# The 1/rms of two stages, taken from the input rows and applied to the projections' products; the rope tables loaded ahead of the gated stage

## The chip, the cores and the metric

The kernel runs on one core of a Trainium2 chip. The metric is device time in microseconds (us), as the median of several executions. The engines of a core work side by side, each through its own instruction queue: PE (TensorE, matrix products and transposes), DVE (VectorE), ACT (ScalarE), POOL (GpSimd) and SP, which here only issues DMA transfers. PEld is PE's loading of weights, which overlaps its products.

## The reference, cut to what matters

A sequence of 256 rows with 1024 features passes a first block (two layers of mixed attention) and a second block (a gated stage, then a dilated attention). Only the second block is touched. In float32:

```
x = first_block(...)
for i in (0, 1):                                  # gated, dilated
    h = x * rsqrt(mean(x*x, axis=-1) + 1e-6) * norm_pre[i]
    y = gated(h) if i == 0 else dilated(h)
    x = x + rms_norm(y) * norm_post[i]

gated(h):    p = h @ w_in                         # 1024 -> 6144
             u, v = split(gelu(p[:, :4096])); z = p[:, 4096:]
             v = layer_norm(v)                    # over 2048
             sv = tril(w_s[g]) @ v + b_s[g]       # per 128 rows, group g of 8
             return (u * sv * silu(z)) @ w_out
dilated(h):  p = h @ w_in                         # 3 groups of q, k, v and one z
             q, k = rope(q, cos, sin), rope(k, cos, sin)
             o_g = softmax(mask(q k / 8)) v; o = sum_g alpha_g o_g
             return (o * silu(z)) @ w_out
```

The factor 1/rms is one number per row of x. A product h @ w has it as a factor per row too.

## The kernel before

**Tiling.** The 256 rows are two row blocks (`tb` 0 and 1) of 128 partitions. A float32 product is made as three matrix products of split numbers: `mm3` (L184) multiplies hi by hi (L193), lo by hi (L194) and hi by lo (L195) for each of 8 pieces of 128 features. Weights arrive by DMA (`raw`, issued by SP at L158), are rounded by ACT (`whi`, L172) and the remainder is taken by POOL (`wlo`, L175) or DVE (`wlo`, L177). SP sends its transfers in the order written.

**From rows to the products' left side.** `make_h_gain` (L257) runs once per row block at each of two boundaries: at the end of the first block (L783) for the gated stage, and at the end of the gated stage (L884) for the dilated one. It takes 1/rms by `row_rstd` (ACT squares and sums the two halves at L232, DVE adds the two sums into `hst` at L234, POOL computes mean plus epsilon at L202 and the power -0.5 at L204). DVE then forms `xh`, the row times 1/rms times the gain, in two halves of 512 (L264). PE transposes each half (`hps`, L269), ACT rounds it to the hi part (`hxh`, L271) and DVE takes the lo part (`hxl`, L272).

**Gated stage** (`gmlp`, L810). Four slabs of v for each block (Gelu at L838, statistics at L839), the layer norm on DVE (L846 to L848), then 8 groups with u (Gelu, L860), z (Tanh of half of it, L862), DVE products at L863 to L866, and the output product.

**Dilated stage** (`dilated`, L888). It loads mask and rope tables at its start. 8 passes (`pair`, L1033) with two heads each: q and k are projected, rotated with the tables (L915 to L917), transposed and split (L924 to L928); v is split in three bf16 parts (`split_v`, L293); z goes through Tanh (L1050) and `gate` (L1052). `attend` (L931) makes scores (L331), masks them with a running maximum (DVE's own instruction at L965), exponentials (L313, with the sum `z`, completed by POOL at L316), transposes them by DMA, multiplies by v (L339 to L341) and divides by z (`rz`, L1018, applied at L1023).

**Order of the work.** In the first two stages the framework's scheduler orders every engine's instructions by its own estimates and the program's dependences; in the dilated stage PE keeps the program's order, which the small planner `Line` (L41) sets by written due times, while the other engines are still ordered by the scheduler. An engine never overtakes within its queue: what waits holds all behind it.

Of the kernel before, what the change touches and what calls it, by code (L numbers as in the profile page):

```python
# [11 lines left out]
F32 = mybir.dt.float32  # L12
# [3 lines left out]
AF = mybir.ActivationFunctionType  # L16
ALU = mybir.AluOpType
# [3 lines left out]
P = 128  # L21
# [94 lines left out]
def tile_kernel(ctx, tc, a, out):  # L116
# [139 lines left out]

    def make_h_gain(tb, act, npre):  # L257

        rs = row_rstd(xs[:, tb, :])
        hi, lo = act  # L260
        t = slice(tb * P, (tb + 1) * P)
        for hf in range(2):
            xh = s512("xh")
            nc.vector.scalar_tensor_tensor(  # L264
                xh, xs[:, tb, hf * 512 : (hf + 1) * 512], rs, npre[hf], ALU.mult, ALU.mult
            )
            ps = bank("tr", "hps", (P, 4, P))
            for j in range(4):
                nc.tensor.transpose(ps[:, j, :], xh[:, j * P : (j + 1) * P], ident)  # L269
            o = slice(4 * hf, 4 * hf + 4)  # L270
            nc.scalar.copy(hi[:, o, t], ps)  # L271
            nc.vector.tensor_tensor(lo[:, o, t], ps, hi[:, o, t].bitcast(F32), ALU.subtract)  # L272

    def row_halves(t, src):

# [14 lines left out]
            lo[:, c0 : c0 + n, t], ps[:, :n, :], scale, hi[:, c0 : c0 + n, t].bitcast(F32), ALU.mult, ALU.subtract  # L290
        )

    def split_v(dst, src, wk, eng=nc.vector):  # L293

        w = src.shape[-1]
        of = lambda t: t.rearrange("p (n m d) -> p n m d", m=dst.shape[2], d=64)
        v1, v2, v3 = (dst[:, :, :, i, :] for i in range(3))
        nc.scalar.copy(v1, of(src))
        r1 = of(wk.tile([P, 256], F32, tag="vr", bufs=1, name="vr")[:, :w])
        eng.tensor_tensor(r1, of(src), v1, ALU.subtract)  # L300
        nc.gpsimd.tensor_copy(v2, r1)
        nc.gpsimd.tensor_tensor(v3, r1, v2, ALU.subtract)

# [43 lines left out]
    def first_block():  # L347
        with ExitStack() as st:
# [327 lines left out]
            for l in range(2):  # L676
# [69 lines left out]
                if l == 0:  # L746
                    for blk in (2, 3):
                        y_out(ya, blk, (7,))
                    ya["x"] = act_tiles("x")
                    for cs_ in ((0, 1, 2, 3), (4, 5, 6)):  # L750
                        for blk in (0, 1):
                            y_out(ya, blk, cs_)
                    for blk in (0, 1):
                        attend(l, 6, "C", S, blk, lam)
                    ws = [load_w(a["w_out"][l, n]) for n in range(2)]
                    gt = gates_of(l, 1)
                    for blk in (2, 3):
                        out_proj(l, blk, ya, ws, gt, residual(l, blk))
                    gtx = gates_of(l, 0)
                    H["c"] = act_tiles("c")  # L760
                    for blk in (2, 3):
                        h_all(1, blk)
                    for blk in (0, 1):
                        y_out(ya, blk, (7,))
                    res = [residual(l, blk) for blk in (0, 1)]
                    for blk in (0, 1):
                        out_proj(l, blk, ya, ws, gtx, res[blk])
                    H["x"] = act_tiles("x")
                    for blk in (0, 1):
                        h_all(1, blk)  # L770
                else:
                    for blk in (0, 1):
                        y_out(ya, blk, (4, 5, 6))
                    gtx = gates_of(l, 0)
                    npre = row_halves(yc[0], a["npre"][0])
                    ws = [load_w(a["w_out"][l, n]) for n in range(2)]
                    hx = x_act()
                    res = [residual(l, blk) for blk in (0, 1)]
                    for blk in (0, 1):
                        attend(l, 6, "C", S, blk, lam)  # L780
                        y_out(ya, blk, (7,))
                        out_proj(l, blk, ya, ws, gtx, res[blk])
                        make_h_gain(blk, hx, npre)  # L783
                    return hx

    def post_add(tb, parts, npost, dst=None):

# [19 lines left out]
        return t  # L807


    def gmlp(hx):  # L810
        with ExitStack() as st:
            pool = lambda name, **k: st.enter_context(tc.tile_pool(name=name, **k))
            wk = pool("gwk", bufs=1)
# [17 lines left out]
            for s, tb in ((0, 0), (1, 0), (0, 1), (1, 1), (2, 0), (2, 1), (3, 0), (3, 1)):  # L831
                    if tb == 0:
                        vws[s] = load_w(a["a_w_in"][s], HALF if s < 2 else PLAIN)
                    w = vws[s]
                    pj = bank("pj", "pj")
                    mm3(pj, hx, tb, w, 0, 512)
                    c = slice(s * 512, (s + 1) * 512)
                    nc.scalar.activation(vn[tb][:, c], pj, AF.Gelu)  # L838
                    nc.vector.bn_stats(st6[tb][:, s, :], vn[tb][:, c])  # L839
            for tb in range(2):  # L840
                mv = sm.tile([P, 2], F32, tag="mv", bufs=2, name="mv")
# [8 lines left out]
            for g in range(8):  # L850
                w = load_w(a["a_w_in"][4 + g])
                for tb in range(2):
                    pj = bank("pj", "pj")
                    mm3(pj, hx, tb, w, 0, 512)
                    sv = bank("sc", "sv", (P, 256))
                    nc.tensor.matmul(
                        sv, ws[:, g, :], vn[tb][:, g * 256 : (g + 1) * 256], start=True, stop=True
                    )
                    gu = wk.tile([P, 256], F32, tag="gu", bufs=2, name="gu")
                    nc.scalar.activation(gu, pj[:, 0:256], AF.Gelu)  # L860
                    tz = wk.tile([P, 256], F32, tag="tz", bufs=2, name="tz")
                    nc.scalar.activation(tz, pj[:, 256:512], AF.Tanh, scale=0.5)  # L862
                    nc.vector.scalar_tensor_tensor(gu, sv, bs[:, g : g + 1], gu, ALU.add, ALU.mult)  # L863
                    nc.vector.scalar_tensor_tensor(tz, tz, 1.0, pj[:, 256:512], ALU.add, ALU.mult)
                    y = wk.tile([P, 256], F32, tag="gy", bufs=2, name="gy")
                    nc.vector.tensor_tensor(y, gu, tz, ALU.mult)  # L866
                    y_to_act([(y[:, i * P : (i + 1) * P], 2 * g + i) for i in range(2)], tb, ya, 0.5)
            npost = row(gp.tile([P, D], F32, name="npost"), a["npost"][0])
            pss = [[bank("sc", "ops")] for tb in range(2)]
            wo = lambda n, kh: load_w(a["a_w_out"][2 * n + kh])  # L870
            for kh in range(2):
                w = wo(0, kh)
# [3 lines left out]
            for tb in range(2):  # L876
                pss[tb].append(bank("pj", "ops"))
                for kh in range(2):
                    mm3(pss[tb][1], ya, tb, w1[kh], 0, 512, k0=8 * kh, first=(kh == 0), last=(kh == 1))
                post_add(tb, [(pss[tb][n], slice(512 * n, 512 * n + 512)) for n in range(2)], npost)  # L880
                if tb == 0:
                    h2 = x_act()
                    npre = row_halves(gp.tile([P, D], F32, name="npre"), a["npre"][1])
                make_h_gain(tb, h2, npre)  # L884
            return h2


    def dilated(hx):  # L888
        with ExitStack() as st:
            pool = lambda name, **k: st.enter_context(tc.tile_pool(name=name, **k))  # L890
            wk = pool("dwk", bufs=1)
            dp = pool("dp", bufs=1)
            mask = dp.tile([P, 1152], F32, name="mask")
            nc.sync.dma_start(mask, a["dmask"])
            rope = {}
            for nm in ("cosD", "sinD"):
                rope[nm] = dp.tile([P, 2, 64], F32, name=nm)
                nc.sync.dma_start(rope[nm], a[nm])
            ya = tuple(dp.tile([P, KC, 256], F32R, name=t) for t in ("yh", "yl"))

            def proj(w, tb, n=512):
# [29 lines left out]
            def attend(pr, tb, qk, v01, v2, gate, lead):  # L931
# [101 lines left out]
            def pair(pr, last):  # L1033
# [5 lines left out]
                def qkv(i, tb):  # L1039
                    pj = proj(ws[i], tb)  # L1040
                    fin = rotate(pj, 512 if i == 0 else 256, tb)
                    if i == 1:
                        split_v(v01[:, :, tb], pj[:, 256:512], wk)
                    turned[i, tb] = line.add(rotate_pe(fin, 4 - 2 * i, tb, qk, 2 * i), 5.0)

                def vz(tb):
                    pj = proj(ws[2], tb, 256)
                    split_v(v2[:, tb : tb + 1], pj[:, :P], wk)
                    tg = wk.tile([P, P], F32, tag="tg", bufs=1, name="tg")
                    nc.scalar.activation(tg, pj[:, P:], AF.Tanh, scale=0.5)  # L1050
# [172 lines left out]
```

## Time and profile before

| what | value |
|---|---|
| median of 3 executions | 1182.47 us (1181.87 to 1186.19) |
| profiled execution | 1193.97 us |
| its span in the trace | 1192.3 us |
| mean granted TensorE clock | 0.954 of full |
| PE busy | 1113.6 us, 93% |
| DVE busy | 837.6 us, 70% |
| ACT busy | 610.5 us, 51% |
| POOL busy | 465.8 us, 39% |
| chain of waits that ended last | PE 79%, DMA 10%, DVE 5%, ACT 2% |

The span is the time from the first to the last instruction in the trace; the profiled execution is 1.67 us longer than it. Busy time of PE is counted as busy at either clock level, so a stretch can be fully busy and still slow. In the timeline, the number in brackets is how long the engine stood idle before the instruction, and the arrow names what ended that. The second block runs from about 652 us to the end.

### The profile page before, as it was taken

The numbers are of one execution on the slowest core, as the hardware profiler recorded it, in microseconds if no ns is written. First come the engines' busy times: TensorE is split into PE (matmuls) and PEld (weight loads), VectorE is DVE, ScalarE is ACT, GpSimd is POOL, SyncE is SP. The second block draws the span as 40 slices with busy tenths as digits, with TensorE's granted clock in tenths as the row PEclk, the third lists the DMA queues.
The fourth block names the chain that finished last, engine by engine and source line by source line (L and its number), as shares of the span: only waits on it lengthen the run. The fifth ranks groups of instructions, "written<-read, shape, count | busy, mean of one in ns | idle before, by whom it ended". The sixth has DMA issues, their size and how long they took to land.

```text
span 1192.3 us, 19339 instructions
## 1 busy us (share of the span) xinstructions
PE 1113.6 (93%) x6600; PEld 851.7 (71%) x6600; DVE 837.6 (70%) x1833; ACT 610.5 (51%) x1364; POOL 465.8 (39%) x698
## 2 busy tenths in 40 slices
PE   5988999898999989999997899999999999999996
PEld 1656657465676777777775688888778888888885
DVE  4467777775476677768876559765568888888783
ACT  2445564554364555566654354554446545555551
POOL 3476655341451039354361301000255555555520
PEclk9989989996999999789999899999989999999998
DMA  9355665878495535666766475555457666876652
GB/s 354 140 146 105 162 146 107 221 141 221 134 235 138 147 128 159 125 106 140 171 161 149 158 245 183 191 170 183 137 179 196 173 178 185 192 173 184 170 144 63
DMA packets 193971, 197.88 MB, mean 166 GB/s; under 512 B 150448, under 2 KB 154576, under 8 KB 193616
## 3 DMA queue, kind: packets, MB, share of 16 engines
q1 hardware_dynamic: 193872, 196.65, 62.0%
q8 instruction: 52, 0.85, 0.3%
q14 instruction: 47, 0.39, 0.1%
HBM read 158.84 MB, written 2.11 MB: 135 GB/s over the span
## 4 chain that ended last, share of the span: by engine, by line
PE 79%; DMA 10%; DVE 5%; issue 2%; ACT 2%; POOL 1%; SPq 0%; DVEq 0%; POOLq 0%; ACTq 0%
PE pj L193 17%; PE pj L194 17%; PE pj L195 16%; PE sc L331 7%; DMA pt<-pp 5%; PE ops L194 3%; PE ops L193 3%; PE ops L195 3%; PE po_bank L339 3%; DMA raw<-in_w_ada 2%; PE po_bank L341 2%; PE adaps L391 2%; DVE wlo L177 1%; PE po_bank L340 1%; PE tp L517 1%
## 5 line engine op out<-in xcount | busy, mean ns | idle before, releaser
L193 PE MATMUL pj<-whi,hxh 128*128 128x512 f32 (+1 forms) x800 | 317.3, 397 | 5.2 <-ACT hxh L271 4.3
L194 PE MATMUL pj<-whi,hxl 128*128 128x512 f32 (+1 forms) x800 | 309.6, 387 | 1.1 <-DVE hxl L255 0.7
L195 PE MATMUL pj<-wlo,hxh 128*128 128x512 f32 (+1 forms) x800 | 307.5, 384 | 0.0
L172 ACT CAST whi<-raw 128x1024 fp32r<-128x1024 f32 x224 | 235.0, 1052 | 139.8 <-DMA raw<-in_b_w_qk 32.5
L175 POOL TENSOR_TENSOR wlo<-raw,whi 128x512 fp32r<-128x512 f32 x130 | 181.6, 1418 | 149.6 <-ACT whi L172 146.5
L177 DVE TENSOR_TENSOR wlo<-raw,whi 128x1024 fp32r<-128x1024 f32 x159 | 202.2, 1275 | 53.5 <-ACT whi L172 52.1
L193 PEld LDWEIGHTS pj<-whi,hxh 128*128 128x128 f32 x800 | 154.3, 193 | 38.4 <-ACT hxh L271 5.0
L194 PEld LDWEIGHTS pj<-whi,hxl 128*128 128x128 f32 x800 | 154.3, 193 | 32.5 <-issue 2.6
L195 PEld LDWEIGHTS pj<-wlo,hxh 128*128 128x128 f32 x800 | 153.4, 192 | 30.3 <-issue 1.1
L313 ACT ACTIVATE pe<-sc,nm 128x512 f32<-128x512 f32 (+2 forms) x184 | 105.3, 576 | 106.9 <-DVE nm L566 51.9
L319 DVE SCALAR_TENSOR_TENSOR pp<-pe,pp 128x512 f16<-128x512 f32 (+3 forms) x152 | 114.8, 760 | 43.4 <-ACT pp L318 42.8
L331 PE MATMUL sc<-qk 64*128 64x256 f32 (+4 forms) x612 | 107.8, 355 | 4.6 <-ACT qk L522 1.9
L318 ACT ACTIVATE pp<-pe 128x512 f16<-128x512 f32 (+3 forms) x152 | 88.6, 590 | 43.2 <-DMA pt<-pp 42.4
L204 POOL TENSOR_TENSOR rs<-ms,mhalf 128x1 f32<-128x1 f32 (+3 forms) x98 | 92.4, 944 | 4.2
L331 PEld LDWEIGHTS sc<-qk 64*128 64x128 f32 (+1 forms) x612 | 64.3, 191 | 39.1 <-issue 13.9
L339 PEld LDWEIGHTS <-pt 128*128 128x128 f16 x544 | 54.0, 99 | 47.0 <-issue 23.2
L193 PE MATMUL pj<-whi,hch 128*128 128x512 f32 (+2 forms) x224 | 81.9, 367 | 0.5 <-ACT whi L172 0.5
L194 PE MATMUL pj<-whi,hcl 128*128 128x512 f32 (+2 forms) x224 | 81.6, 365 | 0.4 <-DVE hcl L255 0.4
L195 PE MATMUL pj<-wlo,hch 128*128 128x512 f32 (+2 forms) x224 | 80.2, 363 | 0.0
L339 PE MATMUL po_bank<-vt,pt 128*128 128x128 bf16 x400 | 67.5, 228 | 13.4 <-DMA pt<-pp 10.4
L341 PE MATMUL po_bank<-vt,pt 128*128 128x128 bf16 x400 | 66.9, 226 | 0.0
L566 DVE TENSOR_REDUCE nm<-sc 128x1 f32<-128x512 f32 (+1 forms) x96 | 54.1, 573 | 18.1 <-PE sc L331 17.6
(192 smaller groups left out, 1963.5 us busy)
## 6 DMA issues: line engine op xcount, KB each, us to landing
raw<-in_b_w_qk SPq DMA_DIRECT2D x64, 512.0 KB, 4.3
raw<-in_w_in SPq DMA_DIRECT2D x56, 512.0 KB, 4.6
raw<-in_w_ada SPq DMA_DIRECT2D x48, 512.0 KB, 4.9
raw<-in_a_w_in SPq DMA_DIRECT2D x48, 512.0 KB, 4.7
raw<-in_w_out SPq DMA_DIRECT2D x16, 512.0 KB, 4.4
raw<-in_a_w_out SPq DMA_DIRECT2D x16, 512.0 KB, 4.6
raw<-in_b_w_vz SPq DMA_DIRECT2D x16, 512.0 KB, 4.1
raw<-in_b_w_out SPq DMA_DIRECT2D x8, 512.0 KB, 3.9
```

What stands on the lines that cost most here:

```text
L172: nc.scalar.copy(hi, raw)
L175: nc.gpsimd.tensor_tensor(lo[:, j], raw[:, j], hi[:, j].bitcast(F32), ALU.subtract)
L177: nc.vector.tensor_tensor(lo, raw, hi.bitcast(F32), ALU.subtract)
L193: nc.tensor.matmul(ps, h, whi[:, c0:c1], start=st, stop=False)
L194: nc.tensor.matmul(ps, l, whi[:, c0:c1], start=False, stop=False)
L195: nc.tensor.matmul(ps, h, wlo[:, c0:c1], start=False, stop=en)
L204: nc.gpsimd.tensor_tensor(rs[:, :n], ms[:, :n], mhalf[:, :n], ALU.pow)
L313: nc.scalar.activation(pe[:, c : c + w], ps, AF.Exp, bias=nm, scale=sign, accum_out=zz)
L319: nc.vector.scalar_tensor_tensor(pp[:, 1, :], pe, PSCALE, pp[:, 0, :], ALU.mult, ALU.subtract)
L331: nc.tensor.matmul(o, q[i == 2], k[i == 1], start=(i == 0), stop=(i == 2))
L339: nc.tensor.matmul(ps, pt[:, 0, i, :], v[:, 0:128], start=(i == 0), stop=False)
L341: nc.tensor.matmul(ps, pt[:, 1, i, :], v[:, 0:128], start=False, stop=(i == n - 1))
```

## The change

`make_h_gain` no longer multiplies by 1/rms: `xh` is the row times the gain (a product of two tensors instead of a combined operation with a factor per row), and `row_rstd` is called behind the transposes. It returns `rs` (1/rms) and `rh`, half of it, made by DVE. The factor is applied to products instead: in the gated stage as the scale of the two Gelus and the Tanh and in the product that makes `y`; in the dilated stage on the rope tables (four products of 128x64), in `split_v` (ACT's copy becomes an Identity with scale; the remainder is one combined operation per head where it was one subtraction for both), as the Tanh's scale, and on `rz` (one product of 128x2 per row block and pass). The rope tables are loaded between the first block and the gated stage.

```diff
     def make_h_gain(tb, act, npre):
-        rs = row_rstd(xs[:, tb, :])
...
-            nc.vector.scalar_tensor_tensor(
-                xh, xs[:, tb, hf * 512 : (hf + 1) * 512], rs, npre[hf], ALU.mult, ALU.mult
-            )
+            nc.vector.tensor_tensor(xh, xs[:, tb, hf * 512 : (hf + 1) * 512], npre[hf], ALU.mult)
...
+        rs = row_rstd(xs[:, tb, :])
+        rh = sm.tile([P, 1], F32, tag="rh", bufs=4, name="rh")
+        nc.vector.tensor_scalar(rh, rs, 0.5, None, ALU.mult)
+        return rs, rh
...
-        nc.scalar.copy(v1, of(src))
+            nc.scalar.activation(v1, of(src), AF.Identity, scale=rs)
...
-        eng.tensor_tensor(r1, of(src), v1, ALU.subtract)
+            for i in range(dst.shape[1]):
+                eng.scalar_tensor_tensor(r1[:, i], of(src)[:, i], rs, v1[:, i], ALU.mult, ALU.subtract)
...
-                    nc.scalar.activation(vn[tb][:, c], pj, AF.Gelu)
+                    nc.scalar.activation(vn[tb][:, c], pj, AF.Gelu, scale=rss[tb][0])
...
-                    nc.scalar.activation(gu, pj[:, 0:256], AF.Gelu)
+                    nc.scalar.activation(gu, pj[:, 0:256], AF.Gelu, scale=rss[tb][0])
...
-                    nc.scalar.activation(tz, pj[:, 256:512], AF.Tanh, scale=0.5)
+                    nc.scalar.activation(tz, pj[:, 256:512], AF.Tanh, scale=rss[tb][1])
...
-                    nc.vector.tensor_tensor(y, gu, tz, ALU.mult)
+                    nc.vector.scalar_tensor_tensor(y, gu, rss[tb][0], tz, ALU.mult, ALU.mult)
...
     # dilated
-            rope = {}
-            for nm in ("cosD", "sinD"):
-                rope[nm] = dp.tile([P, 2, 64], F32, name=nm)
-                nc.sync.dma_start(rope[nm], a[nm])
+            for tb in range(2):
+                for t in rope.values():
+                    nc.vector.tensor_scalar(t[:, tb, :], t[:, tb, :], rss[tb][0], None, ALU.mult)
...
                 nc.vector.reciprocal(rz, z)
+                nc.vector.tensor_scalar(rz, rz, rss[tb][0], None, ALU.mult)
...
-                    nc.scalar.activation(tg, pj[:, P:], AF.Tanh, scale=0.5)
+                    nc.scalar.activation(tg, pj[:, P:], AF.Tanh, scale=rss[tb][1])
...
-    hx = gmlp(first_block())
+    h = first_block()
+    rp = ctx.enter_context(tc.tile_pool(name="rp", bufs=1))
+    rope = {nm: rp.tile([P, 2, 64], F32, name=nm) for nm in ("cosD", "sinD")}
+    for nm, t in rope.items():
+        nc.sync.dma_start(t, a[nm])
+    h = gmlp(*h)
     with tc.manual_schedule(engines={mybir.EngineType.PE}):
-        dilated(hx)
+        dilated(*h, rope)
```

The scheduler answers with another order on DVE, POOL and ACT. On DVE at the first boundary, block 0 (`ov` and the last `xs` are the end of an attention, `yc0` holds the gain), the kernel before has:

```order
L643 TENSOR_TENSOR xs_80<-res_8240,ops_8343 128x512
L595 SCALAR_TENSOR_TENSOR xs_80<-ov_8460,rz_8458,gate_8159 128x64 x2
L234 TENSOR_TENSOR hst_8375<-hss_8370 128x1
L264 SCALAR_TENSOR_TENSOR xh_8381<-xs_80,rs_8379,yc0_99 128x512
L264 SCALAR_TENSOR_TENSOR xh_8390<-xs_80,rs_8379,yc0_99 128x512
L177 TENSOR_TENSOR wlo_8637<-raw_8634,whi_8636 128x1024
L272 TENSOR_TENSOR hxl_8238<-hps_8383,hxh_8237 128x4x128
```

and the changed kernel has:

```order
L652 TENSOR_TENSOR xs_80<-res_8240,ops_8343 128x512
L264 TENSOR_TENSOR xh_8370<-xs_80,yc0_99 128x512
L604 SCALAR_TENSOR_TENSOR xs_80<-ov_8462,rz_8460,gate_8159 128x64 x2
L264 TENSOR_TENSOR xh_8379<-xs_80,yc0_99 128x512
L234 TENSOR_TENSOR hst_8393<-hss_8388 128x1
L177 TENSOR_TENSOR wlo_8648<-raw_8645,whi_8647 128x1024
L273 TENSOR_SCALAR rh_8399<-rs_8397 128x1
L270 TENSOR_TENSOR hxl_8238<-hps_8372,hxh_8237 128x4x128
```

The two `xh` stand ahead of `hst` now, and `hxl` stands behind the new `rh`. On POOL at the same place, the kernel before has:

```order
L302 TENSOR_TENSOR vt_7954<-vr_8162,vt_7954 128x2x64
L175 TENSOR_TENSOR wlo_8590<-raw_8587,whi_8589 128x512 x2
L202 TENSOR_SCALAR ms_8377<-hst_8375 128x1
L204 TENSOR_TENSOR rs_8379<-ms_8377,mhalf_78 128x1
L175 TENSOR_TENSOR wlo_8603<-raw_8600,whi_8602 128x512 x2
```

and the changed one:

```order
L311 TENSOR_TENSOR vt_7954<-vr_8162,vt_7954 128x2x64
L175 TENSOR_TENSOR wlo_8601<-raw_8598,whi_8600 128x512 x2
L202 TENSOR_SCALAR ms_8395<-hst_8393 128x1
L175 TENSOR_TENSOR wlo_8614<-raw_8611,whi_8613 128x512 x2
L204 TENSOR_TENSOR rs_8397<-ms_8395,mhalf_78 128x1
```

The power that makes `rs` stands behind a pair of `wlo` of the weights. On DVE at the second boundary, block 1, with the first rotation of the dilated stage (`t2`, `fin`), the kernel before has:

```order
L234 TENSOR_TENSOR hst_10131<-hss_10126 128x1
L264 SCALAR_TENSOR_TENSOR xh_10137<-xs_80,rs_10135,npre_10030 128x512
L264 SCALAR_TENSOR_TENSOR xh_10146<-xs_80,rs_10135,npre_10030 128x512
L272 TENSOR_TENSOR hxl_10029<-hps_10139,hxh_10028 128x4x128
L272 TENSOR_TENSOR hxl_10029<-hps_10148,hxh_10028 128x4x128
L915 TENSOR_TENSOR t2_10228<-pj_10203,sinD_10169 128x8x32 x2
L916 TENSOR_TENSOR fin_10229<-pj_10203,cosD_10167 128x512
```

and the changed one:

```order
L264 TENSOR_TENSOR xh_10139<-xs_80,npre_10041 128x512
L264 TENSOR_TENSOR xh_10148<-xs_80,npre_10041 128x512
L234 TENSOR_TENSOR hst_10162<-hss_10157 128x1
L925 TENSOR_TENSOR t2_10243<-pj_10218,sinD_8563 128x8x32 x2
L926 TENSOR_TENSOR fin_10244<-pj_10218,cosD_8562 128x512
L270 TENSOR_TENSOR hxl_10040<-hps_10141,hxh_10039 128x4x128
L273 TENSOR_SCALAR rh_10168<-rs_10166 128x1
L908 TENSOR_SCALAR cosD_8562<-cosD_8562,rs_10166 128x64
L908 TENSOR_SCALAR sinD_8563<-sinD_8563,rs_10166 128x64
```

The rotation's first three instructions stand ahead of `hxl` now, and `rh` and the scaling of the tables stand between the two `hxl`.

## Rows read from the trace of the kernel before

**Rows 1.** Windows: us; busy PE, PEld, DVE, ACT, POOL; clock; DMA; GB/s.

```profile
690.00:853.00 163.00, 163.00 (x720) 131.73 (x719) 106.77 (x153) 77.04 (x113) 5.96 (x14) 1.00 0.56 180
...
878.00:903.00 25.00, 24.05 (x145) 20.29 (x145) 17.16 (x29) 12.04 (x20) 13.68 (x12) 1.00 0.52 175
...
903.00:1168.00 265.00, 264.32 (x1823) 220.12 (x1822) 219.14 (x457) 148.17 (x318) 133.32 (x157) 1.00 0.68 174
```

**Rows 2.** The same view, two stretches at the lower clock.

```profile
664.00:667.00 3.00, 3.00 (x8) 2.30 (x7) 0.00 (x0) 0.00 (x0) 0.00 (x0) 0.50 0.66 236
...
865.30:871.70 6.40, 6.27 (x14) 4.61 (x15) 4.25 (x8) 3.85 (x7) 5.41 (x6) 0.50 0.69 214
```

**Rows 3.** Timeline, first boundary, block 0: start, duration, engine, line; brackets: idle, releaser.

```profile
653.31 0.68 DVE L643 TENSOR_TENSOR xs<-res,ops 128x512 f32<-128x512 f32 x1
...
653.91 0.47 DVE L595 SCALAR_TENSOR_TENSOR xs<-ov,rz,gate 128x64 f32<-128x64 f32 x2
...
654.84 0.16 DVE L234 TENSOR_TENSOR hst<-hss 128x1 f32<-128x1 f32 x1 [0.46 <-ACT junk L232]
...
655.89 6.88 POOL L175 TENSOR_TENSOR wlo<-raw,whi 128x512 fp32r<-128x512 f32 x4
...
655.96 3.47 DVE L264 SCALAR_TENSOR_TENSOR xh<-xs,rs,yc 128x512 f32<-128x512 f32 x2 [0.96 <-POOL rs L204]
...
661.56 1.27 DVE L272 TENSOR_TENSOR hxl<-hps,hxh 128x512 fp32r<-128x512 f32 x2
...
662.30 0.33 PE L285 MATMUL yps<-ident,xs 128*128 128x128 f32 x1 [1.87 <-DVE hxl L272]
```

**Rows 4.** Timeline, first boundary, block 1.

```profile
673.94 0.67 DVE L643 TENSOR_TENSOR xs<-res,ops 128x512 f32<-128x512 f32 x1
...
676.58 1.42 DVE L264 SCALAR_TENSOR_TENSOR xh<-xs,rs,yc 128x512 f32<-128x512 f32 x2 [0.96 <-POOL rs L204]
...
678.06 1.28 ACT L838 ACT_TABLE_LOAD   x1 [2.63 <-issue]
...
679.36 1.08 ACT L838 ACTIVATE vn<-pj 128x512 f32<-128x512 f32 x2
...
680.97 1.22 PE L193 MATMUL pj<-whi,hxh 128*128 128x512 f32 x2 [2.20 <-ACT hxh L271]
...
681.99 0.72 PE L194 MATMUL pj<-whi,hxl 128*128 128x512 f32 x1
```

**Rows 5.** Timeline, second boundary, block 0.

```profile
853.28 2.45 DVE L800 SCALAR_TENSOR_TENSOR xs<-otmp,rs,xs 128x512 f32<-128x512 f32 x2
...
859.00 3.46 DVE L264 SCALAR_TENSOR_TENSOR xh<-xs,rs,npre 128x512 f32<-128x512 f32 x2 [0.95 <-POOL rs L204]
...
860.91 1.05 ACT L172 CAST whi<-raw 128x1024 fp32r<-128x1024 f32 x1 [2.70 <-DMA raw<-in_b_w_qk]
...
865.28 0.79 PE L193 MATMUL pj<-whi,hxh 128*128 128x512 f32 x1 [2.05 <-ACT hxh L271]
...
865.46 1.28 DVE L272 TENSOR_TENSOR hxl<-hps,hxh 128x512 fp32r<-128x512 f32 x2
...
866.20 0.79 PE L194 MATMUL pj<-whi,hxl 128*128 128x512 f32 x1
```

**Rows 6.** Timeline, the dilated stage's first rotation and first scores.

```profile
879.67 0.76 DVE L915 TENSOR_TENSOR t<-pj,sinD 128x256 f32<-128x256 f32 x2 [2.75 <-DMA sinD<-in_sinD]
...
899.49 0.44 PE L331 MATMUL sc<-qk 64*128 64x128 f32 x4 [0.82 <-DVE qk L928]
```

**Rows 7.** Groups by line, 903 to 1168 us: busy us, mean ns, idle.

```profile
L177 DVE TENSOR_TENSOR wlo<-raw,whi 128x1024 fp32r<-128x1024 f32 x40 | 49.0, 1226 | 8.6 <-ACT whi L172 8.5
...
L1050 ACT ACTIVATE tg<-pj 128x128 f32<-128x128 f32 x16 | 4.6, 289 | 20.4 <-DVE vr L300 20.4
...
L1052 DVE SCALAR_TENSOR_TENSOR gate<-tg,pj 128x128 f32<-128x128 f32 x16 | 4.5, 281 | 0.1
```

**Rows 8.** Line 252: shortest, median, longest ns.

```profile
L252 ACT ACTIVATE hf<-hps,mcol x32: 445/455/470, 23.7 to 440.4; 128x128 f32<-128x128 f32 x32
```

More of the change, by code (lines that the diff above doesn't have):

```diff
@@ L291, in y_to_act, with split_v @@
         )
-    def split_v(dst, src, wk, eng=nc.vector):
+    def split_v(dst, src, wk, eng=nc.vector, rs=None):
         w = src.shape[-1]
@@ L297, in split_v @@
         v1, v2, v3 = (dst[:, :, :, i, :] for i in range(3))
-        nc.scalar.copy(v1, of(src))
+        if rs is None:
+            nc.scalar.copy(v1, of(src))
+        else:
+            nc.scalar.activation(v1, of(src), AF.Identity, scale=rs)
         r1 = of(wk.tile([P, 256], F32, tag="vr", bufs=1, name="vr")[:, :w])
-        eng.tensor_tensor(r1, of(src), v1, ALU.subtract)
+        if rs is None:
+            eng.tensor_tensor(r1, of(src), v1, ALU.subtract)
+        else:
+            for i in range(dst.shape[1]):
+                eng.scalar_tensor_tensor(r1[:, i], of(src)[:, i], rs, v1[:, i], ALU.mult, ALU.subtract)
         nc.gpsimd.tensor_copy(v2, r1)
@@ L776, in first_block @@
                     ws = [load_w(a["w_out"][l, n]) for n in range(2)]
-                    hx = x_act()
+                    hx, rss = x_act(), []
                     res = [residual(l, blk) for blk in (0, 1)]
@@ L782, in first_block @@
                         out_proj(l, blk, ya, ws, gtx, res[blk])
-                        make_h_gain(blk, hx, npre)
-                    return hx
+                        rss.append(make_h_gain(blk, hx, npre))
+                    return hx, rss
     def post_add(tb, parts, npost, dst=None):
@@ L807, in row, with gmlp @@
         return t
-    def gmlp(hx):
+    def gmlp(hx, rss):
         with ExitStack() as st:
@@ L869, in gmlp @@
             pss = [[bank("sc", "ops")] for tb in range(2)]
+            rs2 = []
             wo = lambda n, kh: load_w(a["a_w_out"][2 * n + kh])
@@ L883, in gmlp, with dilated @@
                     npre = row_halves(gp.tile([P, D], F32, name="npre"), a["npre"][1])
-                make_h_gain(tb, h2, npre)
-            return h2
-    def dilated(hx):
+                rs2.append(make_h_gain(tb, h2, npre))
+            return h2, rs2
+    def dilated(hx, rss, rope):
         with ExitStack() as st:
@@ L1042, in qkv @@
                     if i == 1:
-                        split_v(v01[:, :, tb], pj[:, 256:512], wk)
+                        split_v(v01[:, :, tb], pj[:, 256:512], wk, rs=rss[tb][0])
                     turned[i, tb] = line.add(rotate_pe(fin, 4 - 2 * i, tb, qk, 2 * i), 5.0)
@@ L1047, in vz @@
                     pj = proj(ws[2], tb, 256)
-                    split_v(v2[:, tb : tb + 1], pj[:, :P], wk)
+                    split_v(v2[:, tb : tb + 1], pj[:, :P], wk, rs=rss[tb][0])
                     tg = wk.tile([P, P], F32, tag="tg", bufs=1, name="tg")
-                    nc.scalar.activation(tg, pj[:, P:], AF.Tanh, scale=0.5)
+                    nc.scalar.activation(tg, pj[:, P:], AF.Tanh, scale=rss[tb][1])
                     gates[tb] = wk.tile([P, P], F32, tag=f"gate{tb}", bufs=2, name="gate")
```

## The prediction

> **What bounds the kernel now.** I read the totals first (the table above), then the windows by stage, then the timeline at the two places that the change touches. PE is the bound wherever its inputs are ready: in the gated stage it is busy 163.00 of 163.00 us, in the steady part of the dilated stage 264.32 of 265.00, both at the full clock [rows 1]. There DVE is idle for 56 and 46 us, ACT for 86 and 117. So nothing that only makes DVE or ACT faster or slower can show in these stretches while PE stays fed. What is left in the second block is the two boundaries, where PE waits for the chain row, 1/rms, `xh`, transposes, `hxh`, `hxl`: 1.87 us for `hxl` [rows 3], 2.20 for `hxh` [rows 4], 2.05 for `hxh` [rows 5], and 0.82 before the first scores, with a wait of DVE for the table `sinD` of 2.75 us some 20 us ahead [rows 6]. After the first and the third of these PE runs at the lower of its two clock levels (1.2 in place of 2.4 GHz) for 3.0 and 6.4 us [rows 2].
>
> **First boundary, block 0.** Now: the last `xs` ends at 653.99, and `xh` starts at 655.96, 1.97 us later, since it waits for the sums, the mean and the power; `rs` is there 1.12 us after `hst` began [rows 3]. After: the first `xh` starts at 653.99. I give one `xh` 0.71 us, half of the pair in [rows 4]; beside POOL's `wlo` it took 1.74 [rows 3]. Then 0.47 for the two products that now stand between, and 0.71: `hst` begins at 655.88, 1.04 later than now. `hxl` waits for `rh`, so for the power, so for the pair of `wlo` that POOL now has ahead of it: 655.88 + 1.12 + half of 6.88 (3.44) = 660.44, and 0.16 for `rh` (as `hst`, the nearest of its size) gives 660.60. Before, `hxl` began at 661.56, and PE resumed behind it [rows 3]. Gain 1.0 us. Ends: 0.3, if both `xh` keep their 1.74 beside POOL in part, and 2.0, if the pair of `wlo` starts before `hst` and only its rest counts.
>
> **First boundary, block 1.** `xs` ends at 674.61, `xh` now starts at 676.58 and ends at 678.00; then the table load begins at 678.06 [rows 4]. It is tied to `xh`: the Gelu's output lies in the memory that held the gain, which `xh` reads last. After, `xh` runs from 674.61 to 676.03, the load to 677.4, the first Gelu to 677.9 and, as ACT now alternates Gelu and `hxh`, the first `hxh` to 678.5 (0.54 each by the pair of Gelus in rows 4). On DVE one statistics instruction (put at 0.64, as one `hxl` in rows 3) and `rh` follow the first Gelu: 678.7. The power is long done (`hst` 676.0 + 1.12). `hxl` ends at 679.4, and L194 of PE starts near 679.6 in place of 681.99 [rows 4]. 2.4; I take 2.3. Ends: 0.4, with `xh` at 1.74 each, and 2.6.
>
> **Second boundary.** Block 0: `xs` ends at 855.73, `xh` starts 3.27 later [rows 5]. Without that wait the transposes are early, and what comes last is ACT's cast at 860.91, which waits for a weight transfer and stands ahead of `hxh`: it ends at 861.96, `hxh` at 862.5 (0.54), so L193 starts near 862.6 in place of 865.28. `hxl` stands behind `rh`, two table products and one `wlo` that needs this cast: 861.96 + 1.23 [rows 7] + 0.64 = 863.8 and L194 at 863.9 in place of 866.20 [rows 5]: 2.3. Block 1 gives some back, because two `t2` (0.76, rows 6) and one `fin` now go ahead of its `hxl` on DVE, and they need the last product of block 0. The `fin` has twice the columns of one `t2`, so I put it at 0.7. Of this 1.5 us PE's eight transposes and the `hxh` cover the most; I charge 0.4. Left: 1.9. Ends: 0.5, if all 1.5 and some contention count, and 2.7, the earlier L193.
>
> **Rope tables.** The 2.75 us wait for `sinD` goes, and DVE's weight work behind it comes earlier. I count the later 0.82 us [rows 6]: 0.8, ends 0 and 1.0. The two transfers now stand ahead of the layer norm's tables on SP; these are read after the whole v projection, so I charge nothing.
>
> **Clock.** A stretch at the half clock does half of the work: 1.5 and 3.1 us are lost [rows 2]. The gap of 0.82 us at 899 left the clock at 1.00 in its window [rows 1, 6], and the low stretches came behind gaps of 1.87 and 2.05. After the change I expect gaps of about 0.9 in each place, but in two parts close together, which no row shows. So I take back a fifth, 0.9; ends 0 and 4.6.
>
> **Added work.** In a pass of the dilated stage DVE gets four combined operations of 128x128 for two subtractions, and two products on `rz`: 4 x 0.281 [rows 7] + 2 x 0.16 = 1.44 us at most, with nothing taken off; times 8, 11.5 us against 46 us of idle time. ACT gets 88 scales from a tensor (8 + 16 + 16 gated, 32 + 16 dilated). A row with two such operands takes 455 ns [rows 8], one of the same size without 289 [rows 7], so one is put at 83 ns: 7.3 us together, against 203 us. PE's full business in both stretches is the cover, and I charge 0. If the cover were gone, up to 19 us would show.
>
> The Trainium skill, page "ScalarE: Activation LUTs", section "What ACT_TABLE_LOAD costs", says that each per-partition pointer operand adds about 93 ns to an ACTIVATE; by it the 88 would add 8.2 us to ACT. The rule speaks against the change, the two rows above agree with it within 10 ns, and it is hidden by the same cover.
>
> **Sum.** 1.0 + 2.3 + 1.9 + 0.8 + 0.9 = 6.9 us. The profiled execution would go from 1193.97 to 1187.1. It lies 11.5 us above the median of the runs, so I take the saving off the median: 1182.47 - 6.9 = 1175.6.
>
> **Rivals.** First, the chain only changes its last link: `hxl` still waits, for the power behind `wlo` in block 0 and for the rotation at the second boundary, and the low clock follows as now. Then only block 1 of the first boundary and part of the tables count: 2.3 + 0.5 = 2.8, 1179.7, no change. For it: the new order does put `rh` and the rotation ahead of `hxl`. Against: the times above leave a gain behind these too.
>
> Second, the gaps become short enough that the clock does not fall: 4.6 in place of 0.9, so 10.6 in all, 1171.9. For it: the row at 899. Against: two gaps close together.
>
> Third, on the slow side, one mechanism in the dilated passes: the sum `z` of each pass's second head stands on POOL behind a pair of `wlo` in the new order, and DVE has the reciprocal of it between two parts of the masking of the next scores. If `z` is late by that pair (3.44, rows 3), the softmax is late and PE waits in every pass. 6.9 us are eaten from 0.9 us a pass on; slower by over 0.5% starts at 1.6. With 2.0 a pass: 16 - 6.9, or 1191.6. Against it: PE now idles for 0.68 us in 265 [rows 1], so the due times hold slack, and the `wlo` pair stands behind casts that are mostly early.
>
> **How the numbers follow.** 0.5% of the median, 5.9 us, is about what can be told from no change: 1176.6 to 1188.4. Forecast 0.45, with a range of its own of 1172 to 1179, two thirds of it under 1176.6; first rival 0.25; second 0.20; third 0.10, most of it slower. Faster: 0.30 + 0.20 + 0.01 = 0.51; same: 0.15 + 0.24 + 0.02 = 0.41; slower 0.08. The lowest is the second rival with the good ends, 1168.5; the highest the first rival with a little of the third, 1183. About 1 in 10 is left above, and a little below.
>
> **What would show it.** Right: `xh` of all four blocks starts at the end of `xs`; the table load begins near 676; PE's waits at the boundaries fall from 1.87, 2.20 and 2.05 to about 0.9 or less; no wait before the first scores; 903 to the end as long as now. Wrong: new waits of PE in the dilated passes, `rh` as the releaser of long waits at the boundaries, the first `whi` casts of the dilated weights later than now, or low stretches of the clock in new places.

## The result, and the profile after

| | before | after |
|---|---|---|
| median of 6 executions each | 1183.56 us (1174.92 to 1186.19) | 1164.40 us (1159.59 to 1179.60) |
| ratio | | 0.9854, 95% interval 0.9811 to 0.9896 |
| profiled execution | 1193.97 us | 1175.96 us |
| PE busy | 1113.6 us | 1107.9 us |
| DVE, ACT busy | 837.6, 610.5 us | 840.0, 617.3 us |

The change saved 17 us by the ratio; 6.9 were forecast, and the measured median lies below the range. The profiled execution of the kernel before was a slow one, and the ratios here leave out such executions (the longest, one each of e5 and e7 below, took over 2000 us). A second trace of that kernel took 1183.05 us. So the difference of the two traces, 18 us, must not be read as the gain: 7 of it lie ahead of the last `xs` of the first block, where no instruction was changed and which took from 634 to 654 us over all traces. Two later series of the changed kernel gave 1170.68 us (7 executions; ratio 0.990, 0.9864 to 0.9936) and 1167.95 (6; 0.9899, 0.985 to 0.9947). About 12 us is the better figure; the first interval ends at 12.3.

The same windows as in [rows 1] first (us; busy PE, PEld, DVE, ACT, POOL with counts; clock; DMA; GB/s), of the changed kernel:

```profile
684.00:840.00 156.00, 156.00 (x698) 127.41 (x697) 107.89 (x154) 78.95 (x112) 5.30 (x7) 1.00 0.56 180
...
862.00:887.00 25.00, 25.00 (x138) 21.18 (x137) 14.21 (x28) 12.56 (x17) 14.07 (x12) 0.91 0.57 186
...
887.00:1150.00 263.00, 262.77 (x1831) 220.81 (x1830) 219.58 (x485) 151.14 (x318) 135.38 (x156) 1.00 0.70 175
```

PE is as fully busy as before, DVE and ACT do more work and it does not show. But 698 instructions of PE in 156 us are 223.5 ns each, where [rows 1] has 720 in 163, which is 226.4. That small difference is the term that the prediction did not have; the experiments follow it through the kernel.

The first boundary, block 0, in the timeline of the changed kernel, against [rows 3]:

```profile
646.36 0.68 DVE L652 TENSOR_TENSOR xs<-res,ops 128x512 f32<-128x512 f32 x1
...
646.95 0.69 DVE L264 TENSOR_TENSOR xh<-xs,yc 128x512 f32<-128x512 f32 x1
...
648.55 0.15 DVE L234 TENSOR_TENSOR hst<-hss 128x1 f32<-128x1 f32 x1
...
649.17 3.51 POOL L175 TENSOR_TENSOR wlo<-raw,whi 128x512 fp32r<-128x512 f32 x2 [0.19 <-issue]
...
652.65 0.55 POOL L204 TENSOR_TENSOR rs<-ms,mhalf 128x1 f32<-128x1 f32 x1
...
653.24 0.15 DVE L273 TENSOR_SCALAR rh<-rs 128x1 f32<-128x1 f32 x1 [1.68 <-POOL rs L204]
...
654.04 0.33 PE L287 MATMUL yps<-ident,xs 128*128 128x128 f32 x1 [1.16 <-DVE hxl L270]
```

`xh` starts as soon as `xs` is there, `hst` comes behind it, the power waits for a pair of `wlo`, and `hxl` for `rh` (it starts at 653.31): the chain as predicted. PE waits 1.16 us in place of 1.87. Block 1, against [rows 4]:

```profile
664.06 0.68 DVE L652 TENSOR_TENSOR xs<-res,ops 128x512 f32<-128x512 f32 x1
...
664.66 1.79 DVE L264 TENSOR_TENSOR xh<-xs,yc 128x512 f32<-128x512 f32 x2
...
666.59 1.28 ACT L847 ACT_TABLE_LOAD   x1 [1.04 <-issue]
...
669.10 0.74 PE L193 MATMUL pj<-whi,hxh 128*128 128x512 f32 x2 [0.51 <-ACT hxh L269]
...
670.01 0.50 PE L194 MATMUL pj<-whi,hxl 128*128 128x512 f32 x1 [0.17 <-DVE hxl L270]
```

The table load begins 1.9 us after the end of `xs` (3.5 before), and PE's waits are 0.51 and 0.17 in place of 2.20. Nowhere between 646 and 684 us is the clock below 1.00. The second boundary, block 0, against [rows 5]:

```profile
838.40 2.45 DVE L809 SCALAR_TENSOR_TENSOR xs<-otmp,rs,xs 128x512 f32<-128x512 f32 x2
...
840.77 1.78 DVE L264 TENSOR_TENSOR xh<-xs,npre 128x512 f32<-128x512 f32 x1
...
843.62 0.68 DVE L264 TENSOR_TENSOR xh<-xs,npre 128x512 f32<-128x512 f32 x1
...
845.25 2.52 POOL L175 TENSOR_TENSOR wlo<-raw,whi 128x512 fp32r<-128x512 f32 x2
...
845.39 1.20 DVE L908 TENSOR_SCALAR cosD<-cosD,rs 128x64 f32<-128x64 f32 x1
...
846.51 1.31 DVE L908 TENSOR_SCALAR sinD<-sinD,rs 128x64 f32<-128x64 f32 x1
...
847.75 1.21 DVE L177 TENSOR_TENSOR wlo<-raw,whi 128x1024 fp32r<-128x1024 f32 x1
...
848.88 0.68 DVE L270 TENSOR_TENSOR hxl<-hps,hxh 128x512 fp32r<-128x512 f32 x1
...
847.35 0.49 PE L193 MATMUL pj<-whi,hxh 128*128 128x512 f32 x1 [0.32 <-ACT hxh L269]
...
849.61 0.79 PE L194 MATMUL pj<-whi,hxl 128*128 128x512 f32 x1 [1.77 <-DVE hxl L270]
```

PE waits 1.77 us for `hxl`, which stands behind the two products on the rope tables and a `wlo`. The cast that this `wlo` needs ends at 846.82 and the `wlo` starts at 847.75, behind the products, so by this trace they delay it by 0.9 us; the `wlo` itself is the rest of the chain (e8 below takes the products away). They took 1.20 and 1.31 us beside POOL's `wlo`; the same instruction takes 0.24 when POOL rests, as the next rows show. One `xh`, with two inputs in SBUF, took 1.78 us while POOL worked on a `wlo` (838.70 to 842.00) and 0.68 when it did not. The Trainium skill says that POOL shares its SBUF interfaces with DVE, and that DVE's instructions in a two-port mode or with two SBUF inputs meet contention (page "GPSIMD Engine Reference", section "1. Specifications"); the two `xh` agree with it, and whether the table products, five times as long beside POOL, meet its condition no row shows. Block 1 of the same boundary:

```profile
855.46 3.46 DVE L264 TENSOR_TENSOR xh<-xs,npre 128x512 f32<-128x512 f32 x2
...
860.95 0.24 DVE L908 TENSOR_SCALAR cosD<-cosD,rs 128x64 f32<-128x64 f32 x1
...
857.38 0.63 PE L267 MATMUL hps<-ident,xh 128*128 128x128 f32 x4 [0.83 <-DVE xh L264]
...
859.06 0.69 PE L267 MATMUL hps<-ident,xh 128*128 128x128 f32 x4 [1.05 <-DVE hst L234]
...
861.02 0.80 PE L194 MATMUL pj<-whi,hxl 128*128 128x512 f32 x1 [0.84 <-DVE hxl L270]
```

Here `xh` is late (3.46 us for a pair, beside POOL again), so PE waits for `xh` before each four transposes and then for `hxl`: 0.83, 1.05 and 0.84 us. The kernel before waited 0.23 us for `hxl`:

```profile
876.31 0.50 PE L194 MATMUL pj<-whi,hxl 128*128 128x512 f32 x1 [0.23 <-DVE hxl L272]
```

### The profile page after: what moved, and what is told of

Read it like the earlier page. It is cut to its first block, busy times and chain, and to the rows that moved or that the text cites. A ratio compares the mean times of both kernels' runs of the same rounds, so it can differ in the third digit from the quotient of the medians.

```text
span 1174.2 us, 19375 instructions
## 1 busy us (share of the span) xinstructions
PE 1107.9 (94%) x6600; PEld 854.4 (73%) x6600; DVE 840.0 (72%) x1873; ACT 617.3 (53%) x1364; POOL 470.1 (40%) x698
## 4 chain that ended last, share of the span: by engine, by line
PE 81%; DMA 8%; DVE 4%; ACT 2%; POOL 2%; issue 2%; SPq 0%; DVEq 0%; POOLq 0%; ACTq 0%
PE pj L193 17%; PE pj L194 17%; PE pj L195 17%; PE sc L340 8%; DMA pt<-pp 5%; PE ops L193 3%; PE ops L194 3%; PE ops L195 3%; PE po_bank L348 3%; PE po_bank L350 2%; PE adaps L400 2%; DMA raw<-in_w_ada 2%; PE tp L526 1%; PE po_bank L349 1%; PE yps L287 1%
## 5 line engine op out<-in xcount | busy, mean ns | idle before, releaser
L193 PE MATMUL pj<-whi,hxh 128*128 128x512 f32 (+1 forms) x800 | 313.9, 393 | 2.0 <-ACT hxh L269 1.1
L194 PE MATMUL pj<-whi,hxl 128*128 128x512 f32 (+1 forms) x800 | 304.9, 381 | 3.5 <-DVE hxl L270 2.8
L195 PE MATMUL pj<-wlo,hxh 128*128 128x512 f32 (+1 forms) x800 | 304.2, 380 | 0.0
L175 POOL TENSOR_TENSOR wlo<-raw,whi 128x512 fp32r<-128x512 f32 x130 | 184.5, 1440 | 149.4 <-ACT whi L172 141.6
L194 PEld LDWEIGHTS pj<-whi,hxl 128*128 128x128 f32 x800 | 153.3, 192 | 32.3 <-DVE hxl L270 4.0
L328 DVE SCALAR_TENSOR_TENSOR pp<-pe,pp 128x512 f16<-128x512 f32 (+3 forms) x152 | 110.9, 734 | 38.4 <-ACT pp L327 37.2
L194 PE MATMUL pj<-whi,hcl 128*128 128x512 f32 (+2 forms) x224 | 80.2, 359 | 0.4 <-DVE hcl L255 0.4
L348 PE MATMUL po_bank<-vt,pt 128*128 128x128 bf16 x400 | 68.7, 231 | 9.7 <-DMA pt<-pp 7.0
L350 PE MATMUL po_bank<-vt,pt 128*128 128x128 bf16 x400 | 68.1, 228 | 0.0
```

What stands on the lines that cost most here:

```text
L175: nc.gpsimd.tensor_tensor(lo[:, j], raw[:, j], hi[:, j].bitcast(F32), ALU.subtract)
L193: nc.tensor.matmul(ps, h, whi[:, c0:c1], start=st, stop=False)
L194: nc.tensor.matmul(ps, l, whi[:, c0:c1], start=False, stop=False)
L195: nc.tensor.matmul(ps, h, wlo[:, c0:c1], start=False, stop=en)
L328: nc.vector.scalar_tensor_tensor(pp[:, 1, :], pe, PSCALE, pp[:, 0, :], ALU.mult, ALU.subtract)
L348: nc.tensor.matmul(ps, pt[:, 0, i, :], v[:, 0:128], start=(i == 0), stop=False)
```

## Experiments

Theory A: the change saves some 6 us at the boundaries, and the rest of the difference is spread between executions. Theory B: the changed kernel itself makes PE's steps shorter. Reading the traces, a third and a fourth were formed on the way: C, the step depends on where the products' left sides lie in SBUF (the left side is the piece of 128x128, of `hxh` or `hxl` for instance, that PE loads ahead of a product); D, on something else in the change.

**Each kernel again, and each half of the change alone.** In e3 the second boundary, the dilated stage and the place of the rope tables' loading are those of the kernel before, in e4 the first boundary and the gated stage (`make_h_gain_old` is that function as it was; the scales behind it go too).

```diff
 # e3
-                rs2.append(make_h_gain(tb, h2, npre))
+                rs2.append(make_h_gain_old(tb, h2, npre))
 # e4
-                        rss.append(make_h_gain(blk, hx, npre))
+                        rss.append(make_h_gain_old(blk, hx, npre))
```

> The kernel before, unaltered, a second time with its own profile. Theory A (the change saves some 6 us at the first boundary, the rest of the 18 us between the two profiled executions is spread between executions of any kernel): ratio to the kernel before 1.00 within its interval of about 0.5%, but single executions 10 us apart or more; the time from the span's start to the last xs of the first block differs from 653.3 us by several us, and the step between two 128x512 products at full clock may be 0.229 as in the changed kernel's trace, and not 0.233. Theory B (the changed kernel itself makes PE's steps shorter all over): first block near 653 us and steps of 0.233 again.

> The changed kernel, unaltered, a second time. Theory A: about 6 to 8 us less than before by the median (ratio 0.993 to 0.995), the stretch from the last xs of the first block to the L194 of block 1 23.6 us again (28.7 before), that from there to the end of the span as before within some us, and PE steps of either 0.229 or 0.233. Theory B: ratio 0.985 again, steps 0.229 again and first block near 646 us.

> Only the first boundary and the gated stage are changed; the second boundary, the dilated stage and the place of the rope tables' loading are as before. Theory A: the whole gain of the change, 5 to 7 us (ratio 0.994 to 0.996): first boundary 23.6 us and clock 1.00 in it. Rival (the gain is at both boundaries alike, as predicted): half of it.

> Only the second boundary, the dilated stage and the rope loading are changed; first boundary and gated stage as before. Theory A: same as before within 2 us (ratio 0.998 to 1.002): block 0 gains 1.7 us, block 1 gives it back, first scores come at the same distance from xs of block 0 (44.4 us before, 45.8 in the changed kernel). Rival (as predicted): 2.7 us and the clock's part, ratio 0.996.

| run | median us | ratio to before (95%) | mean step of 128x512 products |
|---|---|---|---|
| e1 | 1179.50 | 0.998 (0.995 to 1.001) | 233.3 ns |
| e2 | 1170.68 | 0.990 (0.9864 to 0.9936) | 230.0 |
| e3 | 1173.76 | 0.9936 (0.9904 to 0.9969) | 229.8 |
| e4 | 1171.14 | 0.9924 (0.9892 to 0.9955) | 229.8 |

The step is the mean distance of the starts of two consecutive 128x512 products at the full clock, over about 2,400 pairs of a trace. Theory A fell: the step is 233.2 to 233.3 in both traces of the kernel before and 229.7 to 230.0 in all four of changed kernels, from the first block on, where their instructions are the same. It belongs to the kernel and not to the execution. What A said of the spread stands: the first block took 647, 645 and 638 us in three traces of the changed kernel (the last is e13's, below), and e2's ratio came out between what A and B expected. And e4, which leaves the first boundary as it was, should have gained nothing by A and gained 0.8%. What e2, e3 and e4 share is `rh`: its four buffers lie in the pool of small tiles, and the built program places `hxh` at byte 106208 of a partition in them, at 106080 in the kernel before. In the changed kernel the output products of the gated stage, whose left side `yh` lies elsewhere, still step at 233.

**The place alone, and the change without it.**

```diff
 # e5: before, plus
+            pad = sm.tile([P, 1], F32, tag="rh", bufs=4, name="rh")
+            nc.gpsimd.memset(pad, 0.0)
 # e6: after, with
-        rs = row_rstd(xs[:, tb, :])
-        rh = sm.tile([P, 1], F32, tag="rh", bufs=4, name="rh")
+        rs, rh = row_rstd(xs[:, tb, :], half=True)
...
 # e8: after, with
-                    nc.vector.tensor_scalar(t[:, tb, :], t[:, tb, :], rss[tb][0], None, ALU.mult)
+                    nc.scalar.activation(t[:, tb, :], t[:, tb, :], AF.Identity, scale=rss[tb][0])
-        nc.vector.tensor_scalar(rh, rs, 0.5, None, ALU.mult)
+        nc.gpsimd.tensor_scalar(rh, rs, 0.5, None, ALU.mult)
```

In e6 `rh` is the next column of the tile that holds `rs`. e7 is the kernel before with the rope tables loaded as in the changed one.

> The kernel before with four unused columns of rh's size taken from the pool of small tiles (128 bytes per partition) and one memset on POOL; no other instruction differs. All later tiles, hx first, lie 128 bytes further, as in the changed kernel. Theory C (the steps between 128x512 products are 229 to 230 ns in place of 233 in every changed kernel because rh moved the products' left sides in SBUF): steps of 229 to 231 from the first block on, 5 to 9 us less than before (ratio 0.992 to 0.996). Theory A (the steps differ by execution) and theory D (by something else in the change): steps 233, ratio 0.998 to 1.002.

> The changed kernel with rh written into a free column of the tile that holds rs, so that no tile ahead of the second block moves. Theory C: steps of 233 again; against before only the boundaries' gain is left, 3 to 5 us (ratio 0.996 to 0.998), with the first boundary at 23.0 us from the last xs of block 0 to the L194 of block 1 (26.4 in the kernel before when its clock stays up). Theories A and D: steps 229 to 231 and ratio 0.988 to 0.992 as for the changed kernel.

> Only the rope tables are loaded ahead of the gated stage. Theory C: steps of 233, the wait before the first scores gone; ratio 0.998 to 1.001. Theory D: steps of 229 to 231 if the loading has to do with it.

> The changed kernel, with the rope tables scaled by ACT and rh made by POOL, so that neither stands ahead of hxl on DVE. Theory C says steps as in the changed kernel (229 to 231). Block 0 of the second boundary: L194 0.9 us earlier (xs to L194 10.3 us, 11.2 in the changed kernel); block 1 of that boundary is held by xh and gains at most that. Ratio to the changed kernel 0.998 to 1.000, to before 0.987 to 0.992. If the tables' scaling cost more than that, 2.5 us less.

| run | median us | ratio to before (95%) | step |
|---|---|---|---|
| e5, place alone | 1174.60 | 0.9959 (0.9924 to 0.9993) | 229.7 ns |
| e6, change without it | 1173.53 | 0.9933 (0.9905 to 0.9961) | 233.3 |
| e7, rope tables alone | 1181.06 | 0.9999 (0.9965 to 1.0033) | 233.2 |
| e8 | 1166.15 | 0.988 (0.9842 to 0.9918) | 229.8 |

Theory C holds in both directions: 128 unused bytes bring the shorter step, and the whole change without them leaves it at 233. Two L194 rows nine products apart, in the timelines of e1, e5, e6 and e11 (below), each at the full clock:

```profile
676.29 0.39 PE L194 MATMUL pj<-whi,hxl 128*128 128x512 f32 x1
...
678.39 0.39 PE L194 MATMUL pj<-whi,hxl 128*128 128x512 f32 x1
```

```profile
669.61 0.39 PE L194 MATMUL pj<-whi,hxl 128*128 128x512 f32 x1
...
671.66 0.39 PE L194 MATMUL pj<-whi,hxl 128*128 128x512 f32 x1
```

```profile
671.51 0.39 PE L194 MATMUL pj<-whi,hxl 128*128 128x512 f32 x1
...
673.61 0.40 PE L194 MATMUL pj<-whi,hxl 128*128 128x512 f32 x1
```

```profile
668.01 0.39 PE L194 MATMUL pj<-whi,hxl 128*128 128x512 f32 x1
...
670.05 0.39 PE L194 MATMUL pj<-whi,hxl 128*128 128x512 f32 x1
```

That is 2.10, 2.05, 2.10 and 2.04 us for nine products, in steps of 233, 228, 233 and 227 ns. The two parts multiply to 0.9933 x 0.9959 = 0.9892, the changed kernel has 0.990: within the intervals they account for the whole. How the gain divides between them is less sure. e6 came out lower than expected (0.996 to 0.998), and the traces divide it the other way, as the end of this part shows.

Where the change proper gains is seen in e1 against e6, both with steps of 233. Windows of e1: the first block, the first boundary, the second boundary up to the second unit of scores, the steady dilated stage:

```profile
0.00:645.44 645.44, 592.43 (x3632) 425.98 (x3633) 447.90 (x1135) 340.76 (x862) 285.30 (x488) 0.94 0.65 163
...
645.44:671.85 26.41, 20.33 (x93) 15.24 (x91) 16.06 (x21) 12.00 (x19) 11.91 (x10) 1.00 0.42 133
...
843.78:897.27 53.49, 47.93 (x244) 37.94 (x242) 37.03 (x61) 29.22 (x53) 28.46 (x30) 0.97 0.58 182
...
897.27:1154.06 256.79, 256.79 (x1787) 214.51 (x1787) 212.96 (x439) 142.75 (x301) 131.84 (x151) 1.00 0.70 176
```

The same stretches of e6:

```profile
0.00:643.47 643.47, 591.33 (x3632) 424.96 (x3633) 453.61 (x1135) 340.31 (x862) 282.39 (x488) 0.93 0.64 164
...
643.47:666.50 23.03, 20.23 (x92) 15.30 (x90) 12.72 (x22) 11.96 (x19) 10.97 (x10) 1.00 0.41 122
...
836.92:891.21 54.29, 49.86 (x242) 40.01 (x240) 39.72 (x71) 30.39 (x54) 30.64 (x32) 0.91 0.56 183
...
891.21:1148.11 256.90, 256.90 (x1787) 214.59 (x1787) 215.34 (x467) 145.56 (x299) 130.88 (x150) 1.00 0.68 175
```

The first boundary is 3.4 us shorter at full clock, the second 0.8 longer, with a mean clock of 0.91 in place of 0.97, and the dilated stage is the same within 0.1. Between the boundaries e6 takes 1.5 us less (170.4, 171.9), since e1 had a low stretch behind the first. From the last `xs` of block 0 to the end it is 3.6 us; the ratio says 7.9 (4.6 to 11.2), and the profiled executions 5.6. The first block, with no changed instruction, differs between 634 and 654 us over the traces, so a single pair of traces can't settle that. The other traces give, from the end of the last `xs` of block 0 to the end of the span:

| kernel (trace) | step | us |
|---|---|---|
| unchanged boundaries (e1; e7) | 233 ns | 535.9; 535.3 |
| change without the place (e6) | 233 | 532.3 |
| place alone (e5) | 230 | 529.3 |
| the changed kernel (first trace; e2; e13) | 230 | 527.2; 526.9; 527.4 |

In this stretch the place is worth 6.6 us without the rest of the change (e1, e5) and 5.1 with it (e6, the mean of the last row), the rest of the change 3.6 at the long step (e1, e6) and 2.1 at the short one. The ratios say 4.8 for the place and 7.9 for the rest. Both parts are there by both ways of counting; the split is not settled.

e8 gained less at the boundary than expected: L194 comes 11.1 us after `xs` began (10.3 expected, 11.2 in the changed kernel), for with nothing else in front, `wlo` itself ran beside POOL and took 1.98, and PE still waited 1.63 us for `hxl`. So it was not the table products alone that held this place:

```profile
841.28 1.98 DVE L177 TENSOR_TENSOR wlo<-raw,whi 128x1024 fp32r<-128x1024 f32 x1 [1.91 <-ACT whi L172]
...
843.18 0.68 DVE L270 TENSOR_TENSOR hxl<-hps,hxh 128x512 fp32r<-128x512 f32 x1
...
843.92 0.52 PE L194 MATMUL pj<-whi,hxl 128*128 128x512 f32 x1 [1.63 <-DVE hxl L270]
```

**How the place acts.** e9 to e12 are e5 with 2, 5, 6 and 8 buffers, one execution each.

> The kernel before with 64 unused bytes per partition instead of 128, so hx lies at 160 of 512 bytes (96 in the kernel before, 224 in the changed one). For the reading of theory C: if a product's step depends on the place of its left side within 128 bytes, steps are another value than 233 (both 96 and 224 are 96 there, so that place alone can't be it); within 256 or 512, open: 229 or 233.

> As e9 with 160 bytes: hx at 256 of 512. Open: 229 or 233; a third level would show that there are more than two.

> As e9 with 192 bytes: hx at 288 of 512, the same place as the weights (whi and wlo lie at 288 of 512 in every kernel). If left and right side disturb each other where their places agree, this is the slowest; otherwise 229 or 233.

> As e9 with 256 bytes: hx at 352 of 512, that is 96 of 256. If the place within 256 bytes decides, 233 as in the kernel before; if the place within 512, open.

Times were 1185.94, 1188.22, 1170.99 and 1178.80 us, beside 1184.53 for the kernel before. The mean steps by the left side's place (`hx` and `hc` move with the padding and are taken together as `hx`; `yh` is the gated stage's `y`, which lies elsewhere; the weights `whi` and `wlo` are at 32 of 256 in all):

| left side's place in 256 bytes | step, ns (kernel and tile) |
|---|---|
| 0 | 233.1 (e10 `hx`), 233.3 (e11 `yh`) |
| 32 | 228.3 (e11 `hx`) |
| 64 | 233.3 (before `yh`, e12 `yh`) |
| 96 | 233.3 (before `hx`), 233.3 (e12 `hx`, at 352 of 512) |
| 128 | 234.2 (e9 `yh`) |
| 160 | 232.5 (e9 `hx`) |
| 192 | 233.3 (after and e5 `yh`) |
| 224 | 229.5 (e5 `hx`), 229.0 (e10 `yh`) |

The place within 256 bytes decides: 96 and 352 agree, 96 and 224 do not, though both are 96 of 128. The expectation of e11 was wrong in its first branch: the place that the weights have too is the fastest.

**A better version.** e14 is the changed kernel with six buffers for `rh`, e15 has e8's edits too and 32 bytes ahead of the gated stage's `yh`.

```diff
 # e14, e15
-        rh = sm.tile([P, 1], F32, tag="rh", bufs=4, name="rh")
+        rh = sm.tile([P, 1], F32, tag="rh", bufs=6, name="rh")
 # e15
             wk = pool("gwk", bufs=1)
+            nc.gpsimd.memset(wk.tile([P, 8], F32, name="ypad"), 0.0)
```

> The changed kernel once more, for comparison on the same chip: ratio to before 0.988 to 0.992, hx at 224 of 256, steps 229 to 230.

> The changed kernel with six buffers for rh in place of four, so that hx lies at 32 of 256 bytes, as in e11, and not at 224. If the place of the left side sets the step independently of the rest of the change (theory C), steps are 228 to 229, 2 to 4 us less than the changed kernel (ratio to before 0.985 to 0.990), and the boundaries' times are those of the changed kernel. If the two do not add up, the ratio stays that of the changed kernel or nears 1.

> As e14, with the rope tables scaled by ACT, rh made by POOL, and 32 bytes ahead of the gated stage's y so that it lies at 32 of 256 too. Theory C: every 128x512 product in the gated and first stage at 228 to 229, about 1 us less than e14 by y and up to 1 us by the boundaries: ratio to before 0.983 to 0.989.

| run | median us | ratio to before (95%) | step |
|---|---|---|---|
| e13, the changed kernel | 1167.95 | 0.9899 (0.985 to 0.9947) | 229.7 ns |
| e14 | 1166.03 | 0.9892 (0.9844 to 0.9939) | 228.7 |
| e15 | 1165.09 | 0.987 (0.9815 to 0.9924) | 228.3 |

In e15 the output products step at 227 where they had 233.3 in e13. The steps follow the place, as C says; of the times only the order does, and e15 is not told apart from e13 by its interval.

## Why the prediction was wrong

**The step that failed is the sum itself: a term was missing.** The prediction counted what the change removes, adds and moves on each engine, and took PE's work in the fully busy stretches as given, "PE's full business in both stretches is the cover". It priced `rh` as 0.16 us on DVE. Its four buffers cost nothing in time, but they shift every later tile, and the products' step falls from 233.3 to 229.7 ns. e5 measures that by itself: 0.41% of the time, 4.8 us (0.8 to 9.0). Whether the other terms together gave their 6.9 us stays open: by e6's ratio they gave 7.9 (4.6 to 11.2), by its trace 3.6, and term by term they did not come out as forecast. A range with any bound on PE's own rate would have been wider; no row of the trace before hinted at it.

**First boundary: right.** Forecast 1.0 + 2.3 us, measured 3.4 between e1 and e6 (1.3 in block 0 and 2.0 in block 1). Even the pair of `wlo` in front of the power was priced well: 3.51 us against 3.44.

**Second boundary: wrong.** With the rope tables 2.7 us were forecast up to the second unit of scores; e6 takes 0.8 longer there than e1. PE's idle time fell by 1.1 us (5.6 to 4.4), and its busy time grew by 1.9, at the lower mean clock. Block 0 came out at 1.9 (forecast 2.3). Block 1 gave back 1.1 in e6 where 0.4 were charged. The chain behind `xh` was expected to be ready before PE; with block 0 shortened it is not, and `xh` beside POOL takes 3.46 us for its two halves, not 1.42.

**Rope tables: the wait is gone, its worth is not shown.** There is no wait before the first scores in the changed kernel. e7 is 0.6 us shorter than e1 from `xs` to the second unit of scores (0.8 forecast), but that is one pair of traces, and its ratio can't show this.

**Clock: too small at one place, wrong in its sign at the other.** The prediction counted low stretches behind the first and the third of the waits that it names. In the same trace there is one behind the second too, of which a part is:

```profile
682.00:684.00 2.00, 2.00 (x6) 1.61 (x6) 0.46 (x1) 0.00 (x0) 0.00 (x0) 0.50 0.96 356
```

A fifth of the loss was to come back. At the first boundary no low stretch was left; in e6 that is the 1.5 us between the boundaries. But the second has more than before (0.91 against 0.97 in e6 and e1), and with it the gap's gain there is gone. In the last 24 to 28 us, where nothing was moved but `rz`, the mean clock is 0.81 in e1, 0.82 in e6 and 0.92 in the changed kernel, so low stretches come and go by more than the gap ahead of them.

**Added work: right.** The steady dilated stage takes 256.8 us in e1 and 256.9 in e6, with all added products and scales in it, and the third rival is refuted with it: PE waits nowhere in it. ACT's busy time grew by 6.7 us between them (7.3 forecast). The second rival's 10.6 us is near the measured 12, but for a wrong reason, the clock: that is luck. Its good ends add up to 12.9 us, which is 1169.6 and not the 1168.5 given as the lowest time.

## What to carry to other kernels

A change that allocates a tile moves the tiles behind it, and here a shift of 128 bytes was worth some 5 us of 12; compare the step of PE's products, in nanoseconds, between two traces before the difference is put down to any wait. To know what a change does by itself, keep the placement fixed or run the placement alone. And where a front chain is shortened, ask at once which chain comes next, and beside which POOL work its DVE instructions will run.

## What was not expected of the hardware

The step of back-to-back 128x512 products depended on where the left side lies within 256 bytes of a partition: 228 to 230 ns at 32 and 224, 232 to 234 at the six other multiples of 32, with the weights at 32 throughout. Whether the left side's own place counts or its distance from the weights was not tried; nor is it known why. In e15 the gated stage's `yh`, at 32 too, stepped at 227. A DVE product of 128x64 with a factor per row took 0.24 us alone and 1.20 to 1.31 beside POOL.
